# Differential attention's last head: a first output group of four products, a later weight split, two norm buffers for the fifth head, earlier diagonals

## The chip, the cores and the metric

The kernel runs on one core of one Trainium2 chip. Its engines are TensorE (PE in the profile, with PEld for its weight loads), VectorE (DVE), ScalarE (ACT), GpSimd (POOL) and SyncE (SP), whose queue issues all transfers of this kernel. The metric is the time of one execution on the device in microseconds, the median of several runs. Lower is better.

## The reference

Two layers over 1024 latent tokens and 256 context tokens of width 1024, all float32: first differential attention with 8 heads, then a state-space layer, each followed by an MLP. The change lies in the attention alone. For each head, two softmaxes over 64 columns each are combined, multiplied with the values and normed; the heads are then projected.

```python
def attend(q, k, v):
    s = jnp.einsum('bqhcd,bkhcd->bhcqk', q, k).astype(jnp.float32)
    p = jax.nn.softmax(s, axis=-1)
    w = p[:, :, 0] - lam * p[:, :, 1]
    o = jnp.einsum('bhqk,bkhe->bqhe', w.astype(v.dtype), v)
    return rmsnorm(o, subln_g) * (1.0 - lambda_init)
...
y_lat = jnp.einsum('bte,ed->btd', o_l, w_o)
```

## The kernel before

Every product of float32 operands is done as three matmuls (`mm3`, L132 to L134) on a high and a low part of each operand; `split` (L137 on ACT, L138 on POOL or DVE) makes the two parts.

`phase_b` is the attention of all heads. It runs through 72 units, n = 9h + u for head h and unit u, and five more that finish the last head. Unit 0 of a head holds the 256 context queries, units 1 to 8 hold 128 latent queries each. Within a manual schedule, the order of PE, DVE, ACT and POOL is the order in which the code calls them; only SP's order is left to a scheduler that simulates the program, as is the order of the sections outside. A unit has these steps, each on the results of the unit before it (`prev`) where it says so:

- `scores` (L579) on PE into banks 0 to 5, `maxima` on DVE (L588, L592), `exps` on ACT (L599, L602), `combine` on DVE (L610, L611, L613).
- The combined weights of the previous unit are transposed on PE in three parts w0, w1, w2 (`w_part`, L620 and L625) into PSUM. A `direct` part is taken out by ACT (L631) and DVE (L632), a `copied` one by ACT (L638) and POOL (L641, L642). `low`, `high` and `whole` name the places in PSUM: `high` is the second half of `low`, and `whole` (columns 1280 to 1792) shares banks 2 and 3 with the scores.
- `values` (PE) after every second unit. `late` is a unit in which values of a pair of query tiles other than the first are due. Then `pair_out` copies (L732), squares on POOL (L733), and `pair_sums` adds up on PE (L740, into the end of `whole`) and ACT (L741).
- Between these steps PE does other products, a group of six or eight (`groups`): projections of the next head's queries and keys for heads 0 to 6 (eight products, table `AHEAD` says in which units), and in the last head and after it `wo_group(i)`, the output projection of token tile i (L858 copies the sum out). The numbers `a`, from `FILLS` or from the lines at L918, say how many products are done at each of three places, `fill(0)` to `fill(2)`: (0, 2, 6, 8) means two, four and two.

`wo_group` takes the first six heads' columns for 512 output columns; heads 6 and 7 follow in `wo_last` (k = 6, 7). Their weights come as four raw pieces (`wload6`), each split on ACT and POOL (`wsplit6`).

The norm of heads 0 to 5 is a detour: the head's output goes to memory (`od`), the scales also (`rsd`), and a later unit loads both (`norm_load`), multiplies on DVE (L775), splits on ACT and POOL and stores (`on`); `beside7` loads the normed heads (`H<-on`). Heads 0 to 4 alternate between two buffers; head 5 uses buffer 1 alone, since buffer 0 lies where `wraw6[2]` is loaded. The last head's norm (`norm7`) makes two diagonal matrices on POOL (L144, L811), which PE multiplies with ones (L815) to spread the scales, before DVE's L817.

## Time and profile before

| what | value |
|---|---|
| median of 3 runs | 2837.14 us (2833.94 to 2844.83) |
| the profiled execution | 2841.76 us, its span 2840.0 us |
| PE busy | 2717.6 us, 96% of the span |
| DVE, ACT, POOL busy | 72%, 48%, 35% |
| units 1 to 76 of `phase_b` | about 231 to 875 us of the span |
| one head of nine units | 76.3 us |
| unit 63 (first of the last head) | scores of this unit at 748.23, of the next at 764.02 us |

Waits are listed as "who waited <- for whom: us in total, times, longest". A row of the timeline has start, duration, engine, line, operation, what it writes and reads, and in brackets the idle time before it and what ended it. In the table of stretches each row gives the busy time of PE, PEld, DVE, ACT and POOL, then the granted clock of PE (1.00 is full), the share of the DMA engines and GB/s. Line numbers are those of the kernel before. `R` and `H` are operands in high and low parts, `F` and `FC` float32 work areas, `W` raw weights and loads, `PS` the PSUM.

### The profile page before, as it was taken

Reading aid. Unit: us, or ns where it says so; the run is one execution under the profiler, and the core shown is the slowest. Engines: PE = TensorE matmul, PEld = TensorE weight load, DVE = VectorE, ACT = ScalarE, POOL = GpSimd, SP = SyncE. Lnnn points to the kernel's source line nnn. Section 1 sums busy time; section 2 is a strip of 40 time slices with the busy share of each in tenths; the row PEclk is TensorE's granted clock in tenths of the full one; section 3 lists DMA queues with packets and bytes.
Section 4 is the critical chain, followed back from the end, with each engine's and each line's share of the span. In section 5 each row is a group of like instructions: output and inputs, shape, how many; then the busy total and the mean of one; then the engine's idle time right before and its main releaser. Section 6 shows DMA issues by size and latency. Waiting matters only on the chain.

```text
span 2840.0 us, 43822 instructions
## 1 busy us (share of the span) xinstructions
PE 2717.6 (96%) x15645; PEld 2257.1 (79%) x15645; DVE 2034.9 (72%) x3029; ACT 1368.8 (48%) x2589; POOL 981.0 (35%) x822
## 2 busy tenths in 40 slices
PE   6999999999899999999999999789999999999999
PEld 4687888888777788778877888788887778878887
DVE  6367888888764667666798877899533697668466
ACT  3425565666554743333444445577444633344443
POOL 3314556556554600000030013688122143235414
PEclk9999999999999999999999999899999999999999
DMA  9954232333516368885799977579642244476544
GB/s 275 322 171 137 66 90 89 94 94 118 171 48 191 119 212 301 301 302 198 275 309 296 289 226 245 182 233 313 217 164 82 71 164 160 152 251 223 168 132 141
DMA packets 377447, 539.12 MB, mean 190 GB/s; under 512 B 38286, under 2 KB 231052, under 8 KB 374028
## 3 DMA queue, kind: packets, MB, share of 16 engines
q1 hardware_dynamic: 377228, 536.32, 58.2%
q8 instruction: 123, 2.02, 0.3%
q14 instruction: 96, 0.79, 0.1%
HBM read 367.54 MB, written 164.47 MB: 187 GB/s over the span
## 4 chain that ended last, share of the span: by engine, by line
PE 55%; DVE 8%; DMA 6%; issue 3%; POOL 2%; ACT 2%; SPq 0%; DVEq 0%; POOLq 0%; ACTq 0%
PE PS L132 16%; PE PS L134 16%; PE PS L133 16%; PE PS L2010 2%; DMA FU<-in_mlp_w 2%; PE PS L2045 2%; DMA Ta<-FU 1%; DMA W<-in_mlp_w 1%; DVE R L138 1%; ACT F L602 1%; DVE H L138 1%; PE PS L579 1%; DVE FD L2019 1%; PE PS L2042 1%; PE PS L1319 0%
## 5 line engine op out<-in xcount | busy, mean ns | idle before, releaser
L132 PE MATMUL PS<-H 128*128 128x512 f32 x1072 | 421.4, 394 | 2.4 <-ACT H L137 2.1
L134 PE MATMUL PS<-H 128*128 128x512 f32 x1072 | 417.9, 390 | 1.9 <-DVE H L2336 1.3
L133 PE MATMUL PS<-H 128*128 128x512 f32 x1072 | 418.2, 390 | 0.0
L132 PE MATMUL PS<-H,R 128*128 128x512 f32 (+1 forms) x828 | 308.0, 374 | 4.1 <-ACT R L137 2.3
L134 PE MATMUL PS<-H,R 128*128 128x512 f32 (+1 forms) x828 | 297.6, 360 | 0.8 <-POOL R L138 0.8
L133 PE MATMUL PS<-H,R 128*128 128x512 f32 (+1 forms) x828 | 298.2, 360 | 0.0
L132 PEld LDWEIGHTS PS<-H 128*128 128x128 f32 x1072 | 201.7, 188 | 50.3 <-issue 6.1
L134 PEld LDWEIGHTS PS<-H 128*128 128x128 f32 x1072 | 201.4, 188 | 45.2 <-DVE H L2336 1.7
L133 PEld LDWEIGHTS PS<-H 128*128 128x128 f32 x1072 | 201.7, 188 | 40.9
L132 PE MATMUL PS<-R,H 128*128 128x512 f32 x534 | 213.6, 401 | 4.0 <-ACT H L137 3.3
L137 ACT ACTIVATE H<-U 128x640 fp32r<-128x640 f32 x216 | 131.8, 674 | 172.6 <-PE PS L133 143.2
L137 ACT ACTIVATE R<-W 128x512 fp32r<-128x512 f32 (+1 forms) x185 | 129.3, 706 | 176.7 <-PE PS L133 102.3
L602 ACT ACTIVATE F<-F,stat 128x1280 f32<-128x1280 f32 x128 | 174.1, 1361 | 82.7 <-DVE F L592 82.6
L134 PE MATMUL PS<-R,H 128*128 128x512 f32 x534 | 211.4, 397 | 1.8 <-DVE H L138 1.8
L133 PE MATMUL PS<-R,H 128*128 128x512 f32 x534 | 210.2, 394 | 0.1
L138 DVE TENSOR_TENSOR H<-U,H 128x640 fp32r<-128x640 f32 x216 | 167.1, 808 | 49.4 <-ACT H L137 48.7
L138 DVE TENSOR_TENSOR H<-W,H 128x512 fp32r<-128x512 f32 (+1 forms) x137 | 123.9, 915 | 103.6 <-ACT H L137 103.2
L592 DVE TENSOR_SCALAR_CACHE_REDUCE F<-PS 128x1280 f32<-128x1280 f32 x128 | 185.2, 1483 | 14.6 <-PE PS L579 14.1
L137 ACT ACTIVATE H<-W 128x512 fp32r<-128x512 f32 (+2 forms) x158 | 95.6, 613 | 188.9 <-PE PS L133 116.9
L132 PEld LDWEIGHTS PS<-H,R 128*128 128x128 f32 x828 | 156.9, 190 | 33.8 <-issue 4.1
L134 PEld LDWEIGHTS PS<-H,R 128*128 128x128 f32 x828 | 156.7, 189 | 26.4 <-POOL R L138 1.0
L133 PEld LDWEIGHTS PS<-H,R 128*128 128x128 f32 x828 | 157.1, 190 | 19.9
(530 smaller groups left out, 6718.7 us busy)
## 6 DMA issues: line engine op xcount, KB each, us to landing
W<-in_mlp_w SPq DMA_DIRECT2D x176, 256.0 KB, 3.3
U<-Aa SPq DMA_DIRECT2D x108, 320.0 KB, 3.8
Aa<-FU SPq DMA_DIRECT2D x91, 320.0 KB, 4.8
Ad<-F SPq DMA_DIRECT2D x112, 256.0 KB, 3.0
W<-Ad SPq DMA_DIRECT2D x112, 256.0 KB, 2.7
FU<-in_mlp_w SPq DMA_DIRECT2D x32, 512.0 KB, 5.8
Ta<-FU SPq DMA_DIRECT2D x16, 1024.0 KB
U<-in_ada_w SPq DMA_DIRECT2D x32, 512.0 KB, 9.3
```

Source lines behind the costliest of these rows:

```text
L132: mm(out, ah, bh, start=first, stop=False, **kw)
L133: mm(out, ah, bl, start=False, stop=False, **kw)
L134: mm(out, al, bh, start=False, stop=last, **kw)
L137: self.nc.scalar.activation(hi, src, AF.Copy)
L138: (lo_eng or self.nc.vector).tensor_tensor(lo, src, hi.bitcast(F32), ALU.subtract)
L579: self.nc.tensor.matmul(self.PS[:, o : o + n], Q[x][r, q0 : q0 + 128], K[y][r, k0 : k0 + n], start=i == 0, stop=i == 2)
L592: ts(p[c], self.PS[:, 1792 * c : 1792 * c + 1280], 1.0, None, ALU.mult, ALU.min, accum_out=sm[:, c : c + 1])
L602: nc.scalar.activation(p[c], p[c], AF.Exp, bias=sm[:, c : c + 1], scale=-1.0, accum_out=sn[:, 0:1] if c else s0[:, u + 1 : u + 2])
L2010: mm(b[:, o : o + 160], X[:, d, i, 64 * j : 64 * j + 128], U[:, 4 * n + i, cols], start=True, stop=True)
L2019: v.tensor_tensor(four(t), x, four(P), ALU.mult)
L2042: mm(o, U[:, 4 * n + i, 32:160], T[:, i], start=True, stop=False)
L2045: mm(o, cs[d][n % 2][j][:, i], W[:, d, i], start=False, stop=d == 1 and j == 1)
```

## The change

No arithmetic is added or removed; products, loads and splits are moved.

1. `wo_group(8)`, the first output group, in unit 63, does four products (k = 0 to 3), all ahead of the transposes; k = 4 and 5 of this tile are done with 6 and 7 in `wo_last`.
2. Raw weights 4 and 5 are loaded in unit 61 (not 60) into the same place as the pieces before them, and split in unit 63, just ahead of L858, the copy of the group's sum (before: at the end of unit 62).
3. Head 5's norm uses both buffers; a pair is still loaded in units 60 to 64, but read one unit later, in 61 to 65.
4. `FILLS` and the default: in unit 0 of a head (4, 2, 2) products in place of (4, 1, 3); in units 5 and 7 (1, 4, 3) in place of (2, 4, 2). In units 69 and 71 two products stand ahead of the first transposes, and the numbers are (2, 3, 1) in place of (0, 3, 3).
5. Tile 6 is summed in bank 4 in place of 7.
6. The diagonals of the last head's pairs 3 and 4 are made sooner, and `wo_last` is called for tiles 8, 9, 0 and then 1 to 4 (before: 8 and 9; 0; 1; 2 to 4, with the norms of pairs 3 and 4 between them at other places).

```diff
-    FILLS = {0: (0, 4, 5, 8), ...
+    FILLS = {0: (0, 4, 6, 8), ...
...
         def norm_load(h, pair):
-            i = 1 if h == 5 else nbuf.next()
+            i = nbuf.next()
...
-        wraw6 = [shaped(self.wv(x, 1024), (2, 512)) for x in (0, 0, 4)]
+        wraw6 = shaped(self.wv(0, 1024), (2, 512))
...
-            b = self.bank(i - 6 if 6 < i < 8 else 7)
+            b, last = self.bank({6: 4, 7: 1}.get(i, 7)), 3 if i == 8 else 5
...
-            return [product(k) for k in range(6)], [out]
+            return [product(k) for k in range(last + 1)], [out]
...
-                for k in (6, 7):
+                k0 = 4 if i == 8 else 6
+                for k in range(k0, 8):
...
-                        a = self.FILLS.get(u, (0, 2, 6, 8))
+                        a = self.FILLS.get(u, (0, 1, 5, 8))
                     else:
-                        a = (0, 4, 4, 6) if u == 0 else (0, 0, 3, 6) if late else (0, 2, 4, 6)
+                        a = (0, 4, 4, 4) if u == 0 else (0, 2, 5, 6) if late else (0, 2, 4, 6)
...
                 def norm():
-                    if front and n - 6 >= 9 and (n - 6) % 9 < 5 and (n - 6) // 9 < 7:
-                        return norm_pair((n - 6) // 9 - 1, (n - 6) % 9)
+                    m = n - 7 if n > 59 else n - 6
+                    if front and m >= 9 and m % 9 < 5 and m // 9 < 7 and n != 60:
+                        return norm_pair(m // 9 - 1, m % 9)
...
-                        if parts == 1:
+                        if parts == 1 or 62 < n < 72:
                             fill(0)
                         w0, w1 = part(0, whole), part(1, high)
...
-                        if n != 73 and parts != 1:
-                            fill(0)
                         fill(1)
...
                     split = norm()
+                if n == 63:
+                    wsplit6(2)
                 if groups:
...
-                todo7, run7 = run7, []
                 if n == 74:
-                    run7.append(list(norm7(tail.pop(0)[1])))
-                    wo_last(8, 9)
+                    diagonals, f = norm7(tail.pop(0)[1])
+                    diagonals()
+                    run7.append([f])
+                    wo_last(8, 9, 0)
+                    todo7 = []
+                else:
+                    todo7, run7 = run7, []
...
-                if n in (58, 61, 62, 72):
-                    wsplit6((58, 61, 62, 72).index(n))
-                if n in (57, 58, 60):
-                    wload6((0, 1, 2)[(57, 58, 60).index(n)])
+                if n in (58, 61, 72):
+                    wsplit6((58, 61, 63, 72).index(n))
+                if n in (57, 58, 61):
+                    wload6((57, 58, 61).index(n))
...
-                    wo_last(*((0,), (1,), (2, 3, 4))[n - 74])
+                    wo_last(*((), (1, 2, 3, 4), ())[n - 74])
...
                 if tail and tail[0][0] == n:
-                    run7.append(list(norm7(tail.pop(0)[1])))
+                    f = list(norm7(tail.pop(0)[1]))
+                    if n == 72:
+                        f.pop(0)()
+                    run7.append(f)
```

Three places show what moves. The first is SP's queue in units 60 to 62, from the store of head 5's scales (`rsd<-F`) on; `F<-rsd` and `W<-rsd` are loads of the scales into the two norm buffers, `H<-on` loads of normed heads, `od` and `on` the detour's stores and loads.

```order
 L80 DMA rsd<-F_1851 10x128
 L80 DMA F_1851<-rsd 128x256
-L80 DMA od<-FC 128x256
-L80 DMA F_1851<-rsd 128x256
-L80 DMA on<-F_1851 128x256
-L80 DMA H<-on 128x512 x3
-L80 DMA on<-F_1851 128x256
-L80 DMA F_1851<-od 128x256
-L80 DMA H<-on 128x256
+L80 DMA W<-rsd 128x256
+L80 DMA od<-FC 128x256
+L80 DMA H<-on 128x512 x10
```

The scales of pairs 0 and 1 are loaded one behind the other, ahead of a run of ten loads of normed heads; before, the second load stood behind the store of an output pair of head 6 and ahead of the stores of the normed pair 0.

The second is ACT's row from the end of unit 62 to the end of unit 63, before the change: the norm's split, the weights' split (R_1850<-W), then unit 63's direct part, exponentials, copies and the group's sum (L858).

```order
L137 ACTIVATE F_1851<-F_1851 128x256
L137 ACTIVATE R_1850<-W 128x1024
L631 ACTIVATE R_110<-PS 128x4x128
L599 ACTIVATE F_1851,FC<-F_1851,stat 128x256 x2
L599 ACTIVATE F_1851,stat<-F_1851,stat 128x256 x2
L638 ACTIVATE F_1851<-PS 128x512
L631 ACTIVATE R_110<-PS 128x2x128
L137 ACTIVATE R_1850<-FC 128x512
L741 ACTIVATE FC<-PS 128x2
L858 ACTIVATE W<-PS 128x512
```

The same stretch with the change:

```order
L137 ACTIVATE W<-W 128x256
L631 ACTIVATE R_110<-PS 128x4x128
L599 ACTIVATE F_1851,FC<-F_1851,stat 128x256 x2
L599 ACTIVATE F_1851,stat<-F_1851,stat 128x256 x2
L638 ACTIVATE F_1851<-PS 128x512
L631 ACTIVATE R_110<-PS 128x2x128
L137 ACTIVATE R_1850<-FC 128x512
L741 ACTIVATE FC<-PS 128x2
L137 ACTIVATE R_1850<-W 128x1024
L858 ACTIVATE W<-PS 128x512
```

The weights' split moved from ahead of unit 63's direct part to right ahead of L858, and the norm's split is now that of pair 1, in the other buffer.

The third is POOL's row in the last units: the split of the last weights (R_110<-W), the square of the last head's pair 4 (L733), the scales and diagonals of pair 3, and the splits of the normed pairs into H.

```order
 L138 TENSOR_TENSOR R_110<-W,R_110 128x1024
-L733 TENSOR_TENSOR adat<-FC 128x256
 L144 TENSOR_TENSOR FC<-FC,mhalf 128x2
 L811 TENSOR_SCALAR FC<-ident,FC 128x128 x2
+L733 TENSOR_TENSOR adat<-FC 128x256
 L138 TENSOR_TENSOR H<-FC,H 128x256
```

The diagonals of pair 3 now stand ahead of the square of pair 4. On PE, the L815 of pair 3 moves ahead of the L740 of pair 4, and 24 matmuls instead of 12 stand between the two L815.

## The prediction

> **What bounds the kernel now.** I read the page first, then PE's waits from 745 to 880 us (the last head and the output products), then a table of stretches of 5 us for the granted clock, then the timeline of single engines around each wait.

> ```profile
> span 2840.0 us, 43822 instructions
> ...
> PE PS L625 <- DVE R L632: 8.5, 4, 6.7
> PE PS L815 <- POOL FC L811: 1.7, 1, 1.7
> ...
> 755.00:760.00 5.00, 0.29 (x2) 0.29 (x3) 3.28 (x11) 2.91 (x8) 3.85 (x5) 0.59 0.70 229
> 760.00:765.00 5.00, 4.88 (x16) 3.73 (x16) 4.86 (x9) 2.83 (x9) 2.79 (x3) 0.50 0.42 112
> 765.00:770.00 5.00, 5.00 (x29) 4.36 (x26) 3.43 (x6) 1.26 (x2) 0.73 (x1) 0.55 0.73 245
> ...
> 840.00:845.00 5.00, 4.47 (x16) 3.17 (x17) 3.41 (x7) 2.77 (x7) 2.67 (x3) 0.66 0.00 0
> ```

> Nearly all of PE's waiting in the changed part is one stall of 6.7 us at unit 63. The clock column (0.59, 0.50, 0.55) adds that PE ran at half rate for 4.1 + 5.0 + 4.5 = 13.6 us around it. Unit 71 has a second half-rate stretch, 0.34 x 5 / 0.5 = 3.4 us. The rows around unit 63, PE first, then DVE, then the queue, ACT and POOL:

> ```profile
> 751.56 0.39 PE L133 MATMUL PS<-R,H 128*128 128x512 f32 x1
> 751.78 0.39 PE L134 MATMUL PS<-R,H 128*128 128x512 f32 x1
> 752.01 1.03 PE L625 MATMUL PS<-ident,F 128*128 128x128 f32 x8
> 759.71 0.69 PE L625 MATMUL PS<-ident,F 128*128 128x128 f32 x2 [6.66 <-DVE R L632]
> 763.25 0.85 PE L740 MATMUL PS<-lamc,adat 128*128 128x1 f32 x4
> 764.02 3.57 PE L579 MATMUL PS<-R 64*128 64x512 f32 x18
> 773.49 0.60 PE L620 MATMUL PS<-ident,F 128*128 128x128 f32 x4
> ...
> 750.20 1.55 DVE L613 SCALAR_TENSOR_TENSOR F<-F,stat 128x1280 f32<-128x1280 f32 x1
> 756.13 0.87 DVE L775 SCALAR_TENSOR_TENSOR F<-F,lamc 128x256 f32<-128x256 f32 x1 [4.38 <-DMA F<-rsd]
> 758.97 0.69 DVE L632 TENSOR_TENSOR R<-PS,R 128x512 fp32r<-128x512 f32 x1 [0.59 <-ACT R L631]
> 765.88 0.17 DVE L840 MEMSET FC<- 128x128 f32 x1
> 767.62 1.49 DVE L592 TENSOR_SCALAR_CACHE_REDUCE F<-PS 128x1280 f32<-128x1280 f32 x1 [1.57 <-PE PS L579]
> ...
> 750.91 0.32 SPq L80 DMA_DIRECT2D F<-rsd  x1
> ...
> 760.80 0.58 ACT L638 ACTIVATE F<-PS 128x512 f32<-128x512 f32 x1
> ...
> 758.53 2.37 POOL L138 TENSOR_TENSOR R<-W,R 128x1024 fp32r<-128x1024 f32 x1 [0.21 <-ACT R L137]
> ```

> The chain: the fifth head's norm (L775) waits 4.38 us for scales whose load was issued at 750.91 through the single buffer. Unit 63's maxima and its L632 stand behind it on DVE, and PE's last two transposes need the half bank that L632 reads.

> **The change, part by part.**

> *Two buffers, norm one unit later; split of weights 4 and 5 moved.* With pairs 0 and 1 loaded right behind the scales and read a unit later, L775 follows L613 directly, at 751.68 in place of 756.13: 4.45 us earlier. The split of 128x1024 leaves ACT's row ahead of L631, so the 0.59 of L632 goes too: 5.04. PE's transposes resume at 759.71 - 5.04 = 754.67. The stall of 6.66 shrinks to 754.67 - 753.04 = 1.6. What is late next: tile 8's last six products (6 x 0.23, spacing of the 751.56 and 751.78 rows) no longer lie between those transposes and the sums, so the sums (L740) reach PE before ACT's copy L638 has read the bank that they write to, and wait for it. L638 stands behind L631 and the exponentials of unit 63, all of which come some 5 us earlier: it ends near 756.1 (761.38 before). From the sums to the scores PE took 764.02 - 763.25 = 0.77 at half rate, 0.4 at full. Unit 64's scores then start near 756.5, not 764.02: 7.5 us. Then two paths meet at the transposes of unit 64 (773.49 before). DVE: it was free at 766.05, now at 761.0; two maxima of 1.4 end at 764.0. PE:

> ```profile
> 810.78 2.00 PE L579 MATMUL PS<-R 64*128 64x512 f32 x18
> 816.41 0.82 PE L625 MATMUL PS<-ident,F 128*128 128x128 f32 x6
> 820.77 0.66 PE L625 MATMUL PS<-ident,F 128*128 128x128 f32 x4 [1.45 <-DVE R L632]
> 838.89 0.44 PE L625 MATMUL PS<-ident,F 128*128 128x128 f32 x2 [0.65 <-DVE F L592]
> 840.30 0.66 PE L625 MATMUL PS<-ident,F 128*128 128x128 f32 x4 [0.97 <-DVE F L592]
> 844.70 0.65 PE L625 MATMUL PS<-ident,F 128*128 128x128 f32 x4 [0.23 <-DVE R L632]
> 848.10 0.50 PE L132 MATMUL PS<-R,H 128*128 128x512 f32 x1 [0.69 <-ACT W L858]
> ...
> 820.03 0.68 DVE L632 TENSOR_TENSOR R<-PS,R 128x512 fp32r<-128x512 f32 x1
> 843.97 0.68 DVE L632 TENSOR_TENSOR R<-PS,R 128x512 fp32r<-128x512 f32 x1
> ```

> The same scores and values took 816.41 - 810.78 = 5.6 us at full clock in unit 69; with 6 x 0.23 more, PE is there at 756.5 + 7.0 = 763.5. So at full clock the gain is 773.49 - 764.0 = 9.5, set by DVE. Each half-rate stretch of 3.4 us takes 1.7 from PE, of which DVE's later arrival hides 0.5 once: one leaves 773.49 - 765.2 = 8.3, two 6.6. Whether the clock falls is the open point. From 752.0 to 756.5 PE now does only transposes and sums, and idles 1.6 ahead of the last two transposes and about 1 ahead of the sums; unit 71 lost its clock with 0.65 + 0.97 of idling. So I take one stretch: **-8.3**, bounds -6.6 and -9.5. [...]

> *Moved transfers.* On SP's queue the scales of pair 1 move ahead of the loads of normed heads (`H<-on`), and the loads of pairs 2 to 4, with the raw weights 4 and 5, stand behind ten of these in one run. POOL and DVE see the same work a unit later. I cost all this at nothing: what hides it is the whole unit that now lies between a pair's load and its L775. Were that cover gone, up to the 4.38 us would return, in unit 63 in place of 62. The loads of the fifth head's normed rows come later too; only the products of weight 5 in unit 64 and after need them, at the end of each group.

> *New wait.* Unit 63's L858 writes its sum where POOL still reads the raw weights 4 and 5. POOL's part of that split (2.37 us) now stands behind its work on unit 63's copy, which can't start before L638 has ended (756.1) and holds two instructions; I put its end near 761 and that of L858 near 762. Unit 64's first products write to the same bank at 756.5 + 5.6 = 762.1. Queued behind L858 on ACT are the norm's split and unit 64's exponentials, whose first maximum is ready at 762.4 anyway. Bounds 0 and 1 us; PE reaches the transposes 0.5 ahead of DVE's 764.0, which covers half of it: 0.

> *Two products ahead of the transposes (units 69 and 71).* Unit 69: L632 (820.03) follows DVE's own combination and ends as before; 6 x 0.23 = 1.38 of PE work, until now behind that wait, fills the 1.45: **-1.4**. Unit 71: the 6 matmuls fill 0.65 and part of 0.97; behind them PE waits for L632 (843.97) as before, but with 3 instead of 9 matmuls left: -1.4 again, whether or not the clock falls, since the wait for L632 takes up what a half-rate stretch costs there. Tile 6 in bank 4 removes the 0.69, the wait for bank 7: together **-2.1**, bounds -0.7 (the bank alone) and -3.6 (the 1.62 of idling, the 0.69, 0.23 and part of the half rate's cost).

> *Tail.*

> ```profile
> 861.43 0.61 POOL L733 TENSOR_TENSOR adat<-FC 128x256 f32<-128x256 f32 x1 [2.53 <-ACT FC L732]
> 862.00 0.71 POOL L144 TENSOR_TENSOR FC<-FC,mhalf 128x2 f32<-128x2 f32 x1
> 868.14 0.73 POOL L138 TENSOR_TENSOR H<-FC,H 128x256 fp32r<-128x256 f32 x1 [4.60 <-ACT H L137]
> 870.42 0.70 PE L815 MATMUL PS<-FC 128*128 128x256 f32 x2 [1.66 <-POOL FC L811]
> ```

> The diagonals of pair 3 stood on POOL behind L733, those of pair 4 behind the pair 3 split at 868.14. Moved ahead, with 24 matmuls (5.5 us) between the two L815, they are ready in time: the 1.66 goes. Tile 8's six matmuls come back here, but they are already out of unit 63's count, so they cost 1.4; with L815 covering the 0.3 that the sums waited for L733: **-0.6**, bounds 0 and -1.9.

> *Fills in all heads.*

> ```profile
> 409.91 1.82 DVE L613 SCALAR_TENSOR_TENSOR F<-F,stat 128x1280 f32<-128x1280 f32 x1
> 412.26 0.60 PE L625 MATMUL PS<-ident,F 128*128 128x128 f32 x4
> 436.70 0.39 PE L132 MATMUL PS<-R 128*128 128x256 f32 x1 [0.69 <-DVE R L632]
> 448.07 0.44 PE L625 MATMUL PS<-ident,F 128*128 128x128 f32 x2 [0.88 <-DVE R L632]
> 462.43 1.49 DVE L592 TENSOR_SCALAR_CACHE_REDUCE F<-PS 128x1280 f32<-128x1280 f32 x1 [0.37 <-PE PS L579]
> ```

> Unit 0: three matmuls (0.69) move into the 0.88 wait, but only the 0.37 that DVE later waits for PE is gained: 6 x -0.37 = -2.2. Unit 5: the transposes would come 0.69 earlier, at 411.57, and meet the end of L613 at 411.73, so 0.2 to 0.3 of stall is new in each of seven heads: +1.7. Unit 7: the shift runs into the 0.69 that PE waits for DVE a unit later: 0. Together **-0.5**, bounds -5 (the whole 0.88 in six heads) and +5 (0.69 lost in each of seven).

> Sum: -8.3 - 1.4 - 2.1 - 0.6 - 0.5 = -12.9. The profiled execution took 2841.76 (span 2840.0 and 1.8 around it), so it would take 2828.9. It lies 4.6 above the median of 2837.14, and its 13.6 us of half rate is what a stall of this length meets when four stretches of 3.4 follow; I estimate that the median execution lost about 2 us less there (one stretch of the four, 1.7). So -11 against the median: **2826**. Also unpriced: the scheduler orders the section after this one (870 to 1100 us) anew, with no product added; I count 0, bounds 3 either way.

> **The rivals.** (1) *All of it*: the clock keeps its rate at units 63 and 71 and DVE's gaps close as well, -9.5 - 1.4 - 3.6 - 1.9 - 2.2 = -18.6, or -16.6 against the median: 2820.5. For it: every gap left is under 1.7 us; against it: unit 71's half-rate stretch. [...] (2) *The stall stays*: the pairs' loads still land late behind the ten loads that they now follow, and L775 waits its 4.38 as before. For it: the row at 750.91 took 5.2 us to land; against it: a unit more of cover. That leaves -1.4 - 2.1 - 0.6 - 0.5 = -4.6: 2832.5. (3) *Slower*: the fills. Transposes put ahead of their data stop PE in units 5 and 7 of all heads, the exponentials follow late, and DVE's chain, which has little slack (the 436.70 wait), grows. It decides once a head loses over 12.9 / 7 = 1.8 us more than I count; at 4 us a head it is 7 x 4 - 12.9 = +15: 2852. For it: DVE is the tighter engine in the heads, as the 0.69 and 0.88 show; against it: in unit 5 L613 ends 0.16 after the earliest new transpose, not 2 us. (4) *Nothing in the end*: the last head is done 13 us sooner, but the section after it, reordered, waits as long as before for its loads; it gives back up to all, 2837. Nothing in the rows above speaks for more than the 3 us named.

> **How the numbers follow.** Forecast 0.53, rival 1 0.27, rival 2 0.10, rival 3 0.05, rival 4 0.05. What a measurement of this kernel can tell from no change is about 0.5%, 14.2 us: faster than 2823, slower than 2851. Rival 1 and 0.05 of the forecast's chance (its lower bounds) fall on faster, 0.32; the rest of the forecast with rivals 2 and 4 on the same, 0.63; rival 3 on slower, 0.05. The range runs from 2816, rival 1 with the fills' better bound, to 2836, rival 2 with the 3 us of the next section.

> **What would show it.** Right: L775 at unit 62 with no DMA wait, PE's gap there under 2 us, one half-rate stretch or none near 756, no L815 wait on POOL over 1 us, unit 70's scores 1.4 us sooner against unit 69's. Wrong: a wait of unit 64's products on L858 over 1 us, new waits of the unit 5 transposes on L613 over 0.5 us a head, or idling on DMA in the section after 870 us that gives the gain back.

## The result and the profile after

| | before | changed |
|---|---|---|
| median (16 runs each) | 2840.09 us | 2833.33 us (2830.39 to 2839.28) |
| ratio of the times | | 0.9979, 95% interval 0.9970 to 0.9988 |
| the profiled execution, its span | 2841.76, 2840.0 us | 2832.56, 2830.8 us |

The changed kernel is 0.21% faster, 6 us (3.4 to 8.5 by the interval); the two profiles differ by 9.2 us. Forecast were 11 us. A second set of runs of the changed kernel gave 0.9978.

The two largest groups of waits of PE in the changed kernel from 740 to 880 us (who waited <- for whom: us, times, longest). The 6.7 us on L632 at unit 63 have become 1.0 (the 1.7 is at unit 71), and the list has no wait for the diagonals (L811) and none for L858 any more:

```profile
PE PS L625 <- DVE R L632: 2.9, 3, 1.7
PE PS L740 <- ACT F L638: 2.3, 3, 1.4
```

The timeline around unit 63, PE first, then DVE:

```profile
755.30 1.03 PE L625 MATMUL PS<-ident,F 128*128 128x128 f32 x8
757.37 0.44 PE L625 MATMUL PS<-ident,F 128*128 128x128 f32 x2 [1.04 <-DVE R L632]
759.17 0.58 PE L740 MATMUL PS<-lamc,adat 128*128 128x1 f32 x4 [1.37 <-ACT F L638]
759.68 3.27 PE L579 MATMUL PS<-R 64*128 64x512 f32 x18
...
754.51 0.83 DVE L775 SCALAR_TENSOR_TENSOR W<-W,lamc 128x256 f32<-128x256 f32 x1
756.63 0.68 DVE L632 TENSOR_TENSOR R<-PS,R 128x512 fp32r<-128x512 f32 x1
759.84 1.61 DVE L613 SCALAR_TENSOR_TENSOR F<-F,stat 128x256 f32<-128x256 f32 x1
761.71 2.52 DVE L138 TENSOR_TENSOR R<-FC,R 128x512 fp32r<-128x512 f32 x1
```

L775 follows its predecessor without a DMA wait. Two small gaps of PE are left, 1.04 and 1.37 us; 1.6 and about 1 were forecast. The scores of unit 64 (L579) take 3.27 us, where those of unit 69 took 2.00 before, and the clock column of the stretches (the number after the five busy times) says why:

```profile
755.00:760.00 5.00, 2.60 (x19) 1.98 (x19) 4.86 (x17) 4.42 (x15) 4.42 (x7) 1.00 1.02 348
760.00:765.00 5.00, 5.00 (x33) 4.29 (x30) 5.00 (x6) 1.84 (x3) 3.68 (x2) 0.66 0.22 72
```

0.34 x 5 / 0.5 = 3.4 us at half rate, one stretch (granted clock 0.66 in the second row) where before had four. At unit 71 the transposes wait 0.45 us for the maxima and 1.67 us for L632, with no half-rate stretch behind them (granted clock 1.00 from 830 to 845 us):

```profile
833.45 0.65 PE L625 MATMUL PS<-ident,F 128*128 128x128 f32 x4 [0.45 <-DVE F L592]
837.85 0.66 PE L625 MATMUL PS<-ident,F 128*128 128x128 f32 x4 [1.67 <-DVE R L632]
...
854.17 0.58 PE L740 MATMUL PS<-lamc,adat 128*128 128x1 f32 x4 [0.67 <-DVE FC L746]
869.81 0.79 PE L133 MATMUL PS<-RT,H 128*128 128x512 f32 x1 [1.83 <-DVE RT L138]
```

The last two rows are the tail: a new wait of the sums (0.67 us), and one of 1.83 us at the start of the next section (`RT` is an operand of that section). And the heads, which were to gain, lost. The combination L613 of the same unit in two heads that follow each other, before and then changed:

```profile
527.96 0.48 DVE L613 SCALAR_TENSOR_TENSOR F<-F,stat 128x256 f32<-128x256 f32 x1
604.33 0.49 DVE L613 SCALAR_TENSOR_TENSOR F<-F,stat 128x256 f32<-128x256 f32 x1
```

```profile
530.79 0.49 DVE L613 SCALAR_TENSOR_TENSOR F<-F,stat 128x256 f32<-128x256 f32 x1
607.47 0.48 DVE L613 SCALAR_TENSOR_TENSOR F<-F,stat 128x256 f32<-128x256 f32 x1
```

76.37 us a head became 76.68.

### The profile page after: what moved, and what is told of

Read it like the earlier page. It is cut to its first block, busy times and chain, and to the rows that moved or that the text cites. A ratio compares the mean times of both kernels' runs of the same rounds, so it can differ in the third digit from the quotient of the medians.

```text
span 2830.8 us, 43820 instructions
## 1 busy us (share of the span) xinstructions
PE 2715.7 (96%) x15645; PEld 2252.6 (80%) x15645; DVE 2039.2 (72%) x3029; ACT 1369.5 (48%) x2589; POOL 975.5 (34%) x822
## 5 line engine op out<-in xcount | busy, mean ns | idle before, releaser
L132 PE MATMUL PS<-H 128*128 128x512 f32 x1072 | 420.6, 393 | 2.4 <-ACT H L137 1.8
L134 PE MATMUL PS<-H 128*128 128x512 f32 x1072 | 417.5, 390 | 3.0 <-DVE H L138 1.7
L133 PE MATMUL PS<-H 128*128 128x512 f32 x1072 | 417.7, 390 | 0.0
L132 PE MATMUL PS<-H,R 128*128 128x512 f32 (+1 forms) x828 | 308.0, 374 | 3.9 <-ACT R L137 2.5
L133 PE MATMUL PS<-H,R 128*128 128x512 f32 (+1 forms) x828 | 298.9, 361 | 0.0
L134 PE MATMUL PS<-H,R 128*128 128x512 f32 (+1 forms) x828 | 298.3, 361 | 0.1
L132 PEld LDWEIGHTS PS<-H 128*128 128x128 f32 x1072 | 201.2, 188 | 50.3 <-issue 6.3
L134 PEld LDWEIGHTS PS<-H 128*128 128x128 f32 x1072 | 201.2, 188 | 46.4 <-DVE H L138 2.5
L133 PEld LDWEIGHTS PS<-H 128*128 128x128 f32 x1072 | 201.3, 188 | 40.4
L132 PE MATMUL PS<-R,H 128*128 128x512 f32 x534 | 212.4, 399 | 3.3 <-ACT H L137 3.3
L137 ACT ACTIVATE R<-W 128x512 fp32r<-128x512 f32 (+1 forms) x185 | 129.2, 706 | 178.5 <-PE PS L133 104.1
L137 ACT ACTIVATE H<-U 128x640 fp32r<-128x640 f32 x216 | 131.9, 674 | 169.9 <-PE PS L133 142.9
L134 PE MATMUL PS<-R,H 128*128 128x512 f32 x534 | 210.8, 396 | 1.9 <-DVE H L138 1.9
L133 PE MATMUL PS<-R,H 128*128 128x512 f32 x534 | 209.4, 392 | 0.0
L138 DVE TENSOR_TENSOR H<-W,H 128x512 fp32r<-128x512 f32 (+1 forms) x137 | 125.9, 930 | 101.9 <-ACT H L137 101.7
L138 DVE TENSOR_TENSOR H<-U,H 128x640 fp32r<-128x640 f32 x216 | 164.9, 797 | 47.3 <-ACT H L137 47.1
L592 DVE TENSOR_SCALAR_CACHE_REDUCE F<-PS 128x1280 f32<-128x1280 f32 x128 | 185.2, 1483 | 12.1 <-PE PS L579 12.1
L137 ACT ACTIVATE H<-W 128x512 fp32r<-128x512 f32 (+2 forms) x158 | 95.3, 613 | 190.3 <-PE PS L133 114.6
L132 PEld LDWEIGHTS PS<-H,R 128*128 128x128 f32 x828 | 157.4, 190 | 33.6 <-issue 4.1
L134 PEld LDWEIGHTS PS<-H,R 128*128 128x128 f32 x828 | 157.5, 190 | 25.4 <-issue 0.8
L133 PEld LDWEIGHTS PS<-H,R 128*128 128x128 f32 x828 | 157.9, 191 | 19.9
```

The costliest lines, as they stand in the source:

```text
L132: mm(out, ah, bh, start=first, stop=False, **kw)
L133: mm(out, ah, bl, start=False, stop=False, **kw)
L134: mm(out, al, bh, start=False, stop=last, **kw)
L137: self.nc.scalar.activation(hi, src, AF.Copy)
L138: (lo_eng or self.nc.vector).tensor_tensor(lo, src, hi.bitcast(F32), ALU.subtract)
L592: ts(p[c], self.PS[:, 1792 * c : 1792 * c + 1280], 1.0, None, ALU.mult, ALU.min, accum_out=sm[:, c : c + 1])
```

## The experiments

Each kernel was timed beside runs of the kernel before on the same chip. Microseconds worked out from a ratio are ratio less 1, times 2837.

**The fills put back.**

```diff
-    FILLS = {0: (0, 4, 6, 8), ...
+    FILLS = {0: (0, 4, 5, 8), ...
...
-    a = self.FILLS.get(u, (0, 1, 5, 8))
+    a = self.FILLS.get(u, (0, 2, 6, 8))
```

> The changed kernel with both tables of where the fills of a unit go as they were before ((0, 4, 5, 8) for unit 0, (0, 2, 6, 8) for units 5, 7 and 8 of all heads); everything in units 57 to 77 stays changed. Theory A (the moved fills cost about 0.3 us in every head, since unit 0's gain comes back in units 1 and 2 and the transposes of units 5 and 7 wait for DVE): one head is 76.3 us again instead of 76.6, unit 63 starts 2 to 3.3 us sooner than in the changed kernel, and the kernel is 2 to 3.3 us faster than it. Rival B (the 0.3 us a head are only this one profile; the fills are neutral): heads within 0.1 us of the changed kernel's, times equal within 0.5 us.

Measured: 2829.13 us, ratio to before 0.9977 (0.9968 to 0.9986), 6.5 us faster. The same two rows of L613:

```profile
529.59 0.49 DVE L613 SCALAR_TENSOR_TENSOR F<-F,stat 128x256 f32<-128x256 f32 x1
605.95 0.48 DVE L613 SCALAR_TENSOR_TENSOR F<-F,stat 128x256 f32<-128x256 f32 x1
```

A head takes 76.36 us again, as theory A has it. From L613 of unit 1 to that of unit 57 this profile takes 473.9 us, the changed kernel 477.0. Unit 57 itself comes only 1.8 us sooner, because unit 1 began 1.3 us later here. The times don't show the 2 to 3.3 us of theory A: the ratios 0.9977 and 0.9979 are 0.6 us apart and can't be told from each other.

**Only units 5 and 7 put back** (the second of the two lines above).

> The changed kernel with only units 5, 7 and 8 back to (0, 2, 6, 8); unit 0 keeps (0, 4, 6, 8). Theory A: unit 0 is 0.7 us shorter and units 1 and 2 are 0.4 and 0.3 longer, as in the changed kernel, so unit 0's move is worth nothing, and units 5 to 8 are as before: heads of 76.3 us, the time of the run with both tables back within 0.5 us. Rival B (unit 0's move gains 0.3 to 0.4 us a head as forecast, and units 5 to 8 alone give it back): heads of 75.9 to 76.0 us, 2 to 3 us faster than the run with both tables back.

Measured: 2831.14 us, 0.9982 (0.9973 to 0.9992).

```profile
529.50 0.48 DVE L613 SCALAR_TENSOR_TENSOR F<-F,stat 128x256 f32<-128x256 f32 x1
605.85 0.48 DVE L613 SCALAR_TENSOR_TENSOR F<-F,stat 128x256 f32<-128x256 f32 x1
```

76.35 us: unit 0's move is worth nothing, and units 5 and 7 cost the whole 0.31 us a head. Rival B, which gave unit 0 a gain of 0.3 to 0.4, falls. The time is 1.4 us over that of the run with both lines put back, within both intervals.

**The fills alone**, both lines changed in the kernel before.

> The kernel before with only the two tables of the fills changed (units 0, 5, 7 and 8 of all heads). Theory A: 0.3 us a head and about 1 us in the first, so 2 to 3.3 us slower than before, the stall of 6.7 us at unit 63 unchanged. My forecast's own step: 0.5 us faster. Rival B (neutral): within 0.5 us.

Measured: 2841.16 us, 1.0013 (1.0004 to 1.0022): 3.7 us slower, 1.1 to 6.2. The forecast's -0.5 is outside. Its heads:

```profile
531.51 0.48 DVE L613 SCALAR_TENSOR_TENSOR F<-F,stat 128x256 f32<-128x256 f32 x1
608.17 0.48 DVE L613 SCALAR_TENSOR_TENSOR F<-F,stat 128x256 f32<-128x256 f32 x1
```

76.66 us. From unit 9 to unit 54 (L613 at 298 and 681 us before), five heads, the three profiles of kernels with both new lines (the changed kernel twice, and this one) lose 2.2 to 2.4 us against before, those with both old lines 0.2 to 0.5, and the one with unit 0's line alone 0.7. From unit 1 to unit 57 the three take 476.9 us on the mean, the eight with both old lines 473.9.

**The norm and the weights alone**, with tile 8's first group of four products, on the kernel before.

```diff
-            i = 1 if h == 5 else nbuf.next()
+            i = nbuf.next()
...
+                    m = n - 7 if n > 59 else n - 6
...
+                if n == 63:
+                    wsplit6(2)
...
-                if n in (57, 58, 60):
+                if n in (57, 58, 61):
```

> The kernel before with only the fifth head's norm on two buffers a unit later, the weights 4 and 5 loaded and split later, and tile 8's first group of four products (its other two at the end). Theory A: the stall of 6.7 us at unit 63 becomes under 2 us, unit 65 starts 8 to 8.6 us sooner, and the tail is 1.4 us longer: 6.6 to 7.2 us faster than before. Rival B (the profile of before met a half-rate stretch more than the median execution, so that the executions gain less): the profile shows the 8 us and the median run only 4 to 5.

Measured: 2834.47 us, 0.9994 (0.9985 to 1.0003): 1.7 us faster, -4.3 to +0.9. Less than either theory, though rival B's 4 us still lie in the interval. The profile shows the stall gone, but a new wait in the place of the old one; PE's rows:

```profile
754.80 0.44 PE L625 MATMUL PS<-ident,F 128*128 128x128 f32 x2 [1.58 <-DVE R L632]
756.29 0.58 PE L740 MATMUL PS<-lamc,adat 128*128 128x1 f32 x4 [1.05 <-POOL W L138]
...
761.26 0.58 PE L132 MATMUL PS<-R 128*128 128x256 f32 x1 [1.57 <-DVE R L632]
```

The values of unit 64 wait 1.57 us for a 128x256 L632 of DVE. The tail takes back part of the gain too: from the last L613 to the next section it took 36.6 us, 33.0 before. Tile 8's six matmuls (1.4 us) are part of it. The wait on the diagonals also grew, from 1.66 to 2.22 us, and the clock was halved behind it for 3.4 us (the two L815 took 1.04 us, 0.70 before):

```profile
866.64 1.04 PE L815 MATMUL PS<-FC 128*128 128x256 f32 x2 [2.22 <-POOL FC L811]
```

**The changed kernel again.**

> The changed kernel once more, unaltered, on the chip of the runs beside it. Theory A (what it gains is -6 us at unit 63, -3.9 at units 69 to 72, about 0 at the tail, +2 to +4 in the heads): 5.5 to 7 us faster than before, and about 2.5 us slower than the run with the old fills was against before (-7.1 on the mean of its runs). Rival B (the true gain is the -9 us of the first pair of profiles): 9 us faster. The profile: heads of 76.6 us again; the number of half-rate stretches at unit 63 is that of chance, one or two.

Measured: 2832.37 us, 0.9978 (0.9969 to 0.9988), 6.2 us faster, as theory A has it. The 2.5 us by which it should trail the run with the old fills do not show in the ratios (0.9978 and 0.9977). Its profile has a span of 2827.6 us, though, 3.2 less than the first one of the same kernel, and a wait that the first did not have. PE, then DVE, then POOL:

```profile
762.59 0.39 PE L132 MATMUL PS<-R 128*128 128x256 f32 x1 [2.45 <-DVE R L632]
...
759.66 2.54 DVE L613 SCALAR_TENSOR_TENSOR F<-F,stat 128x256 f32<-128x256 f32 x1
762.12 0.41 DVE L632 TENSOR_TENSOR R<-PS,R 128x256 fp32r<-128x256 f32 x1
762.46 0.67 DVE L138 TENSOR_TENSOR R<-FC,R 128x512 fp32r<-128x512 f32 x1
...
759.57 2.35 POOL L138 TENSOR_TENSOR R<-W,R 128x1024 fp32r<-128x1024 f32 x1
```

The second part of the moved split (POOL, 2.35 us) began 0.09 us ahead of L613, which took 2.54 us in place of 0.48 and ended 0.28 us after it. In the first profile L613 met POOL's L642 (1.61 us), and L138 met the split: 2.52 us in place of 0.67. So in each of the two profiles one DVE instruction takes 1.9 to 2.1 us longer beside the split, L138 in the first and L613 in the second; PE's wait of 2.45 us is in the second alone. The old place was not free either: there L537 met the same subtraction (POOL, from 758.53 to 760.90 us). Before, then changed (first profile):

```profile
759.57 1.87 DVE L537 TENSOR_TENSOR FC<-FC 128x512 f32<-128x512 f32 x1
```

```profile
757.24 0.97 DVE L537 TENSOR_TENSOR FC<-FC 128x512 f32<-128x512 f32 x1
```

From unit 63's L632 to the memset L840, DVE's whole chain took 6.91 us before and 7.97 and 8.10 in the two profiles of the changed kernel. With the split at the old place it was 6.9 to 7.8 in four profiles, so the move itself costs DVE about 0.2 to 1.2 us.

**Units 69 and 71 alone**, on the kernel before.

```diff
-    a = ... (0, 0, 3, 6) if late ...
+    a = ... (0, 2, 5, 6) if late ...
...
-                        if parts == 1:
+                        if parts == 1 or 62 < n < 72:
                             fill(0)
```

> The kernel before with only the two products ahead of the transposes in the late units (64 to 71) and the last head's tile 6 in bank 4. Theory A (my forecast's steps): unit 69 to 70 is 1.4 to 1.6 us shorter, unit 71 to 72 2.1 to 2.3 us, the stall of 6.7 us at unit 63 stays: 3.5 to 3.9 us faster. Rival B (the time comes back at the next wait, DVE's): the profile shows the shorter units and the section after 870 us starts less than 1 us sooner; within 1 us.

Measured: 2834.96 us, 0.9990 (0.9979 to 1.0000): 2.8 us faster. By L613 unit 69 to 70 is 1.64 us shorter, and by L632 unit 71 to 72 2.31, as in the changed kernel (1.63 and 2.34):

```profile
840.64 0.66 PE L625 MATMUL PS<-ident,F 128*128 128x128 f32 x4 [0.44 <-DVE F L592]
845.04 0.66 PE L625 MATMUL PS<-ident,F 128*128 128x128 f32 x4 [1.67 <-DVE R L632]
```

Theory A by the profile; the interval of the times (0 to 6.0 us faster) holds both theories.

**The tail alone**, on the kernel before.

```diff
-                    run7.append(list(norm7(tail.pop(0)[1])))
-                    wo_last(8, 9)
+                    diagonals, f = norm7(tail.pop(0)[1])
+                    diagonals()
+                    run7.append([f])
+                    wo_last(8, 9, 0)
```

> The kernel before with only the order of the tail changed: diagonals of pairs 3 and 4 made sooner, tiles 8, 9 and 0 ahead of the last sums, tiles 1 to 4 in one go. Tile 8 keeps its six products in unit 63, so its six matmuls (1.4 us) do not return here. Theory A: the wait of 1.7 us on the diagonals goes, a wait of about 0.7 us on the sums of pair 3 is new: 1.0 to 1.6 us faster where the clock stays at full rate. My forecast's step: 0.6 + 1.4 = 2.0 us faster. Rival B (PE's wait moves to the chain of the last pair): 0 within 0.4 us.

Measured: 2836.38 us, 0.9995 (0.9985 to 1.0005): 1.4 us faster, not told from none. The profile: from the last L632 to the next section 1.15 us less, as theory A has it. The wait on the diagonals is gone, and a new one stands on the sums, behind the smaller DVE work of the pair:

```profile
859.27 0.58 PE L740 MATMUL PS<-lamc,adat 128*128 128x1 f32 x4 [0.66 <-DVE FC L746]
```

**More work for PE at unit 63**, on the kernel with the fills put back. The group's first product starts the sum in its bank anew (`start` in L132), so of a group begun twice only the second round counts; all else is as it was.

```diff
+                    if n == 63:
+                        fills = [groups[0][0] + groups[0][0][0:2], groups[0][0][2:4], []]
```

> The changed kernel with the old fills, and in unit 63 PE has more to do: the four products of tile 8 are begun, the first two of them twice (the second start overwrites the bank, so the result is the same) and the last two repeated behind the transposes: 12 matmuls of 128x512 more, 2.8 us, in a place where PE waited 2.6 us in two gaps of 1.6 and 1.1. Theory A (the clock is halved for the 3.4 us that follow a window of a fixed 3.4 us grid in which PE streamed for less than 0.43 of the time; the gaps are too short by any other count): no half-rate stretch at 750 to 770 us in place of two, and unit 65 starts 1 to 2.5 us sooner against unit 63 than with the old fills alone; 1 to 2 us faster than it. Rival B (the half rate has another cause, or DVE bounds unit 64 anyway): the added matmuls only delay the sums, 0 to 1 us slower than the run with the old fills.

Measured: 2827.46 us, 0.9963 (0.9948 to 0.9978): 10.5 us faster than before, on six runs. The stretches, first with the fills put back alone, then with the added products:

```profile
755.00:760.00 5.00, 3.08 (x14) 2.57 (x16) 4.86 (x11) 4.12 (x13) 4.58 (x6) 0.67 0.87 275
760.00:765.00 5.00, 5.00 (x32) 4.50 (x31) 5.00 (x7) 1.44 (x3) 2.84 (x2) 0.65 0.14 45
```

```profile
755.00:760.00 5.00, 3.76 (x24) 3.04 (x22) 4.17 (x16) 3.89 (x13) 3.37 (x5) 1.00 0.91 276
760.00:765.00 5.00, 4.90 (x43) 4.42 (x43) 4.96 (x5) 2.04 (x4) 4.11 (x3) 1.00 0.16 58
```

Two half-rate stretches in a row (clock 0.67 and 0.65) became none. From L613 of unit 57 to that of unit 66 this profile takes 78.3 us, 1.1 less than with the old fills alone (79.4), with twelve matmuls more whose result is thrown away. That is the low end of theory A; and the first profile of the changed kernel, with one half-rate stretch, took no longer (78.2). The ratio is 4 us better than the old fills' 0.9977, more than theory A's 1 to 2, but the two intervals overlap.

**The same again**, to see whether that was chance.

> The kernel with the old fills and the busier unit 63 once more, unaltered. Theory A (a window in which PE streams for more than 0.43 of the time keeps the clock): again no half-rate stretch between 740 and 800 us, and 9 to 10.5 us faster than before. Rival B (the first profile met no half-rate stretch there by chance): one or two of 3.4 us at 755 to 765 us, and 7 us faster, as with the old fills alone.

Measured: 2827.48 us, 0.9954 (0.9940 to 0.9968), and again no half-rate stretch between 740 and 800 us. Theory A, though these 13.1 us (9.1 to 17.0) are more than its 9 to 10.5. The median of this kernel is the one it had (2827.46, 2827.48); that of the kernel before, beside it, was 2837.57 in the first set and 2841.34 in the second. A ratio carries this scatter too.

**The subtraction of the moved split on DVE**, on top of it.

```diff
-            self.split(hi, lo, ..., nc.gpsimd)
+            self.split(hi, lo, ..., nc.vector if j == 2 else nc.gpsimd)
```

> The kernel with the old fills and the busier unit 63, and the second half of the split of weights 4 and 5 (the subtraction of 128x1024) on VectorE in place of GpSimd. In the profiles so far this subtraction takes 2.4 to 2.6 us on GpSimd, and the VectorE instruction from SBUF that meets it ends only with it: the 128x512 subtraction takes 2.5 in place of 0.67 us, or a 128x256 combination 2.5 in place of 0.5, behind which PE's values once waited 2.45 us. Theory A (the two engines exclude each other on SBUF operands): no VectorE instruction of unit 63 is stretched beyond 1.4 us there, the subtraction takes about 1.3 us on VectorE, the maxima of unit 64 begin 0.5 to 1.7 us sooner against the section's start, no wait of 2 us and more for the values; but PE has few gaps left, so the kernel is only 0 to 1 us faster. Rival B (those instructions are stretched by something else): 2.5 us again, and 1.3 us slower on VectorE.

Measured: 2827.23 us, 0.9955 (0.9942 to 0.9967), no different from the kernel without it. DVE's rows with the split on POOL, with POOL's own behind them, and then on DVE:

```profile
761.79 2.54 DVE L138 TENSOR_TENSOR R<-FC,R 128x512 fp32r<-128x512 f32 x1
...
761.21 2.58 POOL L138 TENSOR_TENSOR R<-W,R 128x1024 fp32r<-128x1024 f32 x1
```

```profile
761.46 0.67 DVE L138 TENSOR_TENSOR R<-FC,R 128x512 fp32r<-128x512 f32 x1
762.46 1.21 DVE L138 TENSOR_TENSOR R<-W,R 128x1024 fp32r<-128x1024 f32 x1
```

Both subtractions on DVE took 1.88 us, less than the smaller one beside POOL (2.54). Theory A was too strict in one number: an L613 still took 1.62 us, beside POOL's L642 (1.30 us). The maxima of unit 64 came 0.5 to 0.7 us sooner, and so little reaches the end.

## Why the prediction was right or wrong

Twelve profiles now show the last head. The stretch from L613 of unit 57 to that of unit 66, and the time at half rate in it:

| kernel | us | at half rate |
|---|---|---|
| before | 86.84 | 13.7 |
| fills alone; units 69 and 71 alone; tail alone | 85.7; 84.8; 84.8 | 10.2 each |
| changed, twice | 78.2; 79.8 | 3.4 each |
| old fills; units 5 and 7 put back; norm and weights alone | 79.4; 79.9; 80.4 | 6.8 each |
| busier unit 63, twice; with the split on DVE | 78.3; 78.3; 77.8 | 0 |

- *Unit 63 (-8.3, less 2 for the median): right.* In the pair of profiles it was -8.7. Against the mean of the four with the old unit 63 (85.5) it was -6.5. The profile of before had met one half-rate stretch more than the other three with the same unit 63, as the two microseconds of allowance assumed. (The 4.6 us that the profile lay above the median of 3 runs were not that: above the median of 16 it lay 1.7.) As a kernel of its own, with the 1.4 us of the tail, this step should have given -4.9; it was timed at -1.7 (-4.3 to +0.9), and the longer tail of that run accounts for part of the difference.
- *POOL and DVE see the same work a unit later, at nothing: wrong.* At its new place POOL's split makes a DVE instruction 1.9 to 2.1 us longer; less what the old place cost, DVE loses 0.2 to 1.2 us. From L613 of unit 62 to the memset L840, DVE gained 3.8 us in the pair of profiles, not the 5.04 of the forecast. In the second profile PE then waited 2.45 us for DVE, in the run of the norm and weights alone 1.57.
- *New wait on L858 (0): right.* No such wait of PE is in the changed kernel's list.
- *Units 69 and 71 (-1.4, -2.1): right*, -1.6 and -2.3 in every kernel that has them.
- *Tail (-0.6): about 0.* The wait of 1.66 us went and the 1.4 us of matmuls came, as said; the 0.67 us of the sums behind L746 was not foreseen. The section after it starts with a wait on DVE's L138 of 0.7 to 1.8 us in the changed kernel and those built on it, and of 0.2 with the tail alone. The four kernels with the old tail, before among them, have none; why it varies is open.
- *Fills in all heads (-0.5): the step that failed.* It measured about +3 us in the profiles (unit 1 to unit 57) and +3.7 us as a kernel of its own. The part that was wrong is unit 0's -2.2: with only unit 0's line new (second experiment) a head took 76.35 us, 76.36 with neither, so it was worth nothing. The +1.7 of unit 5 was nearly right: units 5 and 7 cost 0.31 us a head, 2.2 us in seven. I let three matmuls of unit 0 move into the 0.88 us wait and booked the 0.37 us that DVE later waits for PE as the gain. The changed rows of units 0 and 1 (PE):

```profile
450.54 0.44 PE L625 MATMUL PS<-ident,F 128*128 128x128 f32 x2 [0.18 <-DVE R L632]
455.00 0.39 PE L132 MATMUL PS<-R 128*128 128x256 f32 x1 [0.38 <-DVE R L632]
```

  The wait did shrink to 0.18, and on PE unit 0 became 0.70 us shorter; units 1 and 2 became 0.43 and 0.28 longer. First, the values of unit 1 now wait 0.38 us for an L632 of DVE, whose time has not moved. Then the scores of unit 2 begin sooner and take longer, 2.14 us before and 2.43 changed, and DVE's maxima wait for them as they did:

```profile
460.27 2.14 PE L579 MATMUL PS<-R 64*128 64x512 f32 x18
```

```profile
462.45 2.43 PE L579 MATMUL PS<-R 64*128 64x512 f32 x18
464.92 1.49 DVE L592 TENSOR_SCALAR_CACHE_REDUCE F<-PS 128x1280 f32<-128x1280 f32 x1 [0.38 <-PE PS L579]
```

  In both profiles the thirteenth of these 18 matmuls waits for another L632 of DVE and starts within 0.05 us of its end. From L613 of unit 8 to that of unit 1 DVE took 15.44 us before and 15.46 changed. DVE waited for a PE that was itself held by DVE: a loop, in which nothing was to be had. Unit 5 was right (0.3: its transposes now follow L613's end by 0.14 us, by 0.53 before), but unit 7 also lost 0.34, which unit 8 (-0.36) repaid.
- *The rivals.* The clock did not keep its rate by itself (1; 3.4 us at half rate in both profiles), the norm did not wait for its loads (2). Rival 3 had the right sign for the fills and a tenth of the size. The section after 870 us gave nothing back (4): it took 1964.8 us before and 1964.6 changed. Over the twelve profiles it took 1958.5 to 1965.2 us, with no shift between kernels with the old and the new tail that stands out of this scatter.

Sum of what was measured: -6.5 - 1.6 - 2.3 + 0 + 3 (the fills, between 2.2 and 3.7) = -7.4, against -6.0 (-8.5 to -3.4) timed. The parts as kernels of their own add to -1.7 + 3.7 - 2.8 - 1.4 = -2.2, with an uncertainty of about 5; they don't contradict the sum, and don't settle it to a microsecond. The fills are the largest miss of a term, but the times don't show that they are all of it. With the old fills the forecast's other terms come to -10.4 against the median, and that kernel was timed at -6.5 (-9.1 to -4.0). Where the rest went stays open.

A version that beats both is the changed kernel with the old fills and the busier unit 63: 0.9963 and 0.9954 in two sets of runs, 10 to 13 us faster than before.

## What to carry to other kernels

Before filling a wait, follow its releaser one round further back: if that engine is in turn held by the one that is to be relieved, the wait is a loop and moves to the next unit. Two profiles of one kernel differed by 3 us in span, so a change of a few microseconds is read from the same stretch in several profiles, with the half-rate time beside each. Where half-rate stretches follow a wait of PE, repeated products in the gap may be cheaper than the gap: in the last three experiments' profiles, at this one place, none was left, against 6.8 us at half rate with the old fills alone, and the stretch took 77.8 to 78.3 us against 79.4.

## What the runs showed of the hardware

```profile
753.23:756.65 3.42, 3.10 (x18) 2.44 (x16) 3.42 (x11) 1.15 (x4) 3.34 (x4) 1.00 0.97 287
756.65:760.06 3.41, 1.32 (x10) 1.06 (x12) 3.27 (x10) 3.41 (x13) 2.92 (x5) 1.00 1.02 358
760.06:763.47 3.41, 3.41 (x21) 2.72 (x18) 3.41 (x3) 0.84 (x1) 3.41 (x2) 0.50 0.30 99
```

In the second profile of the same kernel the grid lies elsewhere. The same two gaps, 1.44 and 1.05 us there, were shared by two windows (0.53 and 0.60 streamed), and the clock stayed. Only the third window, with the 2.45 us wait in it (0.24 streamed), was followed by a halved one.

```profile
752.80:756.21 3.41, 1.97 (x14) 1.53 (x13) 3.41 (x12) 2.08 (x7) 3.24 (x4) 1.00 1.01 356
756.21:759.62 3.41, 2.36 (x18) 1.88 (x20) 3.30 (x6) 3.15 (x9) 3.31 (x5) 1.00 0.86 297
759.62:763.04 3.42, 0.97 (x11) 0.76 (x8) 3.38 (x4) 0.60 (x1) 2.30 (x1) 1.00 0.02 6
```

With the added products no window there was below 0.54, and the granted clock was 1.00 from 750 to 770 us in both runs.

*DVE and POOL.* In the rows above, some DVE instructions that don't read PSUM took longer beside a split or copy of POOL, and ended 0.28 to 0.55 us after it. L613 (128x256) took 2.54 us beside the split and 1.61 beside L642, for 0.48; L138 (128x512) 2.52 and 2.54 beside the split, for 0.67; L537 1.87 beside the split at its old place, for 0.67. L632, which reads PSUM, took 0.69 us beside that same split; all its 112 rows in the profile of before lie between 0.41 and 0.69. Not every one of POOL's instructions went with a longer one of DVE: at 417 us of the changed kernel an L537 of 0.67 us ended 0.97 us ahead of an L144 (128x10, 1.97 us) that had begun 0.33 us before it, and L144 of this shape took 1.95 to 1.99 us in all seven rows of both profiles. With the split on DVE, L138 was back at 0.67; what makes these rows longer beside POOL, no run here shows. By them the moved split, which I had put at nothing, costs one DVE instruction of unit 63 between 1.9 and 2.1 us.
